# Two MoE layers on one core: the second step's gate and up products moved right behind the first step's, and the expert order found earlier

## The chip, the cores and the metric

One Trainium2 chip, one of its cores. The metric is device microseconds of one execution, as the median over runs; smaller is better.

## What is computed

A trunk of two residual layers over 256 tokens of width 1024, in float32. Layer 0 mixes tokens by a convolution module, layer 1 by differential attention. Each mixer is followed by a mixture of 32 gated-MLP experts (four groups of eight; every token takes the best group and in it two experts), and then by a gated per-layer embedding. The mixture, cut to what matters:

```python
for g in range(N_GROUPS):
    hg = jnp.einsum("bsd,edf->bsef", h, w_gate[g])
    ug = jnp.einsum("bsd,edf->bsef", h, w_up[g])
    act = jax.nn.silu(hg) * ug * combine[:, :, g, :, None]
    out = out + jnp.einsum("bsef,efd->bsd", act, w_down[g])
```

One expert has 3 MB of weights: gate 1024x256, up 1024x256, down 256x1024. All 32 experts of both layers are read, some 200 MB of the 244 MB that the kernel reads.

## The kernel before, in words

**Steps.** The function `moe` (from L1024) works through the experts in steps: in layer 0 eight steps of four experts with 32 token places each; in layer 1 eight steps of two experts with 64 places (one of them shares its step in quarters) and four of four. In layer 1 a place stands not for a fixed expert but for a rank of load: experts are sorted by their counts, so that crowded ones get more places. The first six experts have fixed places (three steps); which expert stands at a later place is found on the chip.

**One step u on TensorE**, in program order: `gate_up(u)` (L1138: the products of its experts with gate and up, in two halves over eight channels), `slots(u)` (L1111, L1115: weights and positions by place), `finish_up(u)` (ACT L1147, DVE L1149: silu times up), half of the `dispatch` of a later step pair (L1076: tokens gathered by a product with the one-hot matrix S, written out by ACT L1081), `combine(u-1)` (L1184), `turn(u)` (L1157, L1159: transposes), `down(u)` (L1170). In the first step of a layer, other work is written between the two halves of `gate_up(0)`: `weights` (L583 to L602), `counts` (L569, L575, and ACT L577, L578), the second half of the first dispatch, and in layer 1 `places_of` (L631 to L643: the sort on DVE). Behind the second half, layer 1 has `by_place` (L649 to L668: ranks, counts and weights are rearranged by place, and the sorted list of experts is written to `row`), then the weight stream is released and `overflow` is prepared.

**The weight stream.** All large weights come through one ring of 16 slots of 1 MB, in one fixed list of tiles, all issued from SP's queue (class `Stream`, L144 to L238). A gate/up tile holds half of the channels of one expert's gate and up (two DMAs of 0.5 MB), a down tile the whole of its down weights. The list is in the order of the steps as they were: a step's gate/up tiles, its down tiles, the next step's gate/up tiles. Slots are handed on strictly in that order:

```python
    while self.used in self.over:
        self.used += 1
    self.fill()
```

so a tile read out of order gives its slot to nobody until all tiles listed ahead of it are read too. Three half tiles of each layer's first step lie in extra buffers (`early`) outside the ring. Counted from a layer's first expert tile, the list is:

- layer 0: tiles 1 to 5 gate/up of step 0, 6 to 9 its down; 10 to 17 gate/up of step 1, 18 to 21 its down; 22 to 29 gate/up of step 2, and so on, twelve a step.
- layer 1: tile 1 gate/up of step 0, 2 and 3 its down; 4 to 7 gate/up of step 1, 8 and 9 its down; 10 to 15 step 2; tiles 16 to 19 gate/up of step 3, 20 and 21 its down; 22 to 25 gate/up of step 4, and so on. From tile 16 on the expert is found by the sort: the list is held there (`W.held`) until `by_place` has written `row`, which SP then reads into a register (L257).

Tile n + 16 can be issued when tiles 1 to n have been read. Other lines used below: L438 `warm` (products for nothing, to keep TensorE going), L552 `low` (DVE: the low parts of the tokens, in halves), L560 `ranks`, L601 and L602 `split_weights`.

Of the kernel before, what the change touches and what calls it, by code (L numbers as in the profile page):

```python
# [10 lines left out]
F32 = mybir.dt.float32  # L11
# [4 lines left out]
AF = mybir.ActivationFunctionType  # L16
# [3 lines left out]
P = 128  # L20
T = 256
D = 1024
NC8 = 8
NE = 32
# [31 lines left out]
RW = ((6, 4), (4, 4))  # L56
# [33 lines left out]
def kernel(  # L90
# [7 lines left out]
    nc = tc.nc  # L98
# [5 lines left out]
    work = ctx.enter_context(tc.tile_pool(name="work", bufs=1))  # L104
# [5 lines left out]
    def ps_b(name="psb"):  # L110
        return psum.tile([P, 512], F32, tag="b", name=name, bufs=2)
# [128 lines left out]
    W = Stream()  # L240
# [107 lines left out]
    ident = const.tile([P, P], F32, name="ident")  # L348
# [85 lines left out]
    def warm(n):  # L434

        ps = ps_b("warm") if n else None
        for _ in range(n):
            nc.tensor.matmul(ps, ones_bf, before[:, None, :].to_broadcast([P, 4, P]), start=True, stop=True)  # L438
# [10 lines left out]
    def routing(i):  # L449


        R = Routing()
# [4 lines left out]
        both = range(2)  # L457
# [9 lines left out]
        cnt = t([P, NE], F32, "cnt")  # L467
# [96 lines left out]
        def counts():  # L564
            pst = ps_b()
            for tt in range(2):
                for t in range(tt + 1):
                    for n in range(2):
                        nc.tensor.matmul(pst[0:NE, tt * P:(tt + 1) * P], oh[:, t, n],  # L569
                                         before_off if t == tt else ones_bf, start=(t == 0 and n == 0),  # L570
                                         stop=(t == tt and n == 1))
            pcn = ps_b()
            for t in range(2):
                for n in range(2):
                    nc.tensor.matmul(pcn[:, 0:NE], ones_bf, oh[:, t, n], start=(t == 0 and n == 0),  # L575
                                     stop=(t == 1 and n == 1))
            nc.scalar.activation(srT, pst[0:NE, 0:T], AF.Copy)  # L577
            nc.scalar.activation(cnt, pcn[:, 0:NE], AF.Copy)  # L578

        def weights():  # L580

# [62 lines left out]

        def by_place():

            pt = ps_b()
            for tt in both:
                nc.tensor.transpose(pt[0:NE, tt * P:(tt + 1) * P], wgt[:, tt], ident)  # L649
            wT = work.tile([NE, T], F32, tag="sq", name="wgtT", bufs=1)  # L650
            nc.scalar.activation(wT, pt[0:NE, 0:T], AF.Copy)
            pm = ps_b()
            for tt in both:
                nc.tensor.matmul(pm[:, tt * NE:(tt + 1) * NE], srT[:, tt * P:(tt + 1) * P], R.permb[:, 0], start=True,
                                 stop=True)
            nc.tensor.matmul(pm[:, 2 * NE:4 * NE], ones_bf[0:NE], R.permb[:, 1:3].rearrange("e a r -> e (a r)"),
                             start=True, stop=True)
            for tt in both:
                nc.tensor.matmul(pm[:, (4 + tt) * NE:(5 + tt) * NE], wT[:, tt * P:(tt + 1) * P], R.perm, start=True,
                                 stop=True)  # L660
            row = t([1, NE], I32, "row")
            nc.vector.tensor_copy(row, pm[0:1, 3 * NE:4 * NE])
            order["row"] = row
            nc.vector.tensor_copy(sr.rearrange("p t e -> p (t e)"), pm[:, 0:2 * NE])
            R.of = late([P, NE], F32, "of")
            nc.scalar.activation(cnt, pm[:, 2 * NE:3 * NE], AF.Copy)
            nc.scalar.activation(R.of, pm[:, 3 * NE:4 * NE], AF.Copy)
            nc.scalar.activation(wgt.rearrange("p t e -> p (t e)"), pm[:, 4 * NE:6 * NE], AF.Copy)  # L668
            split_weights()

        def overflow():
# [15 lines left out]

        R.prepare, R.gather, R.rows, R.logits, R.pick, R.low = prepare, gather, rows, logits, pick, low
        R.ranks, R.counts, R.weights, R.overflow = ranks, counts, weights, overflow
        R.place_constants, R.places_of, R.by_place = place_constants, places_of, by_place  # L690
        return R

    class Pools:
# [22 lines left out]
    pools = [Pools(i) for i in range(2)]  # L716
# [307 lines left out]
    def moe(i, R, between):  # L1024
# [4 lines left out]
        with ExitStack() as ctx:  # L1029
# [54 lines left out]
            def dispatch_first(tt, c0, c1):  # L1084

                if tt == 0 and c0 == 0:
                    hgs[0] = big_t("hg")
                    start.extend(ps_d()[:, 0:256] for _ in range(4))
                for xx in (R.xh, R.xl):
                    for c in range(c0, c1):  # L1090
                        nc.tensor.matmul(start[c], xx[tt][:, c], Ss[0][:, tt],
                                         start=(tt == 0 and xx is R.xh), stop=(tt == 1 and xx is R.xl))
                for c in range(c0, c1):
                    if tt == 1:
                        nc.scalar.activation(hgs[0][:, c], start[c], AF.Copy, scale=g_ffn[:, c:c + 1])
# [111 lines left out]
                dispatch_first(0, 0, 4)  # L1207
            warm(RW[i][0])
            R.ranks(1)
            warm(RW[i][1])  # L1210
            spots(0, (1,))
            R.low(1, 0)
            dispatch_first(1, 0, 4)
            R.low(1, 1)
            for u in range(ns + 1):
                q = u // 2 + 1
                if u == max(OVER_AT[i] - 1, 0):
                    W.ahead = OVER_AHEAD[i]
                if u < ns:
                    gate_up(u, 0, 4)  # L1220
                    if u == 0:
                        R.weights()
                        R.counts()
                        if i == 0:
                            spots(1)
                        dispatch(0, 1)
                        if i:
                            R.places_of()
                        else:
                            R.overflow()  # L1230
                    gate_up(u, 4, 8)
                    if u == 0:
                        pools[i].rest()
                        ep = pools[i].second
                        if i:
                            R.by_place()
                            spots(1)
                            W.held = None
                            W.fill()
                            R.overflow()  # L1240
                    slots(u)
                    finish_up(u)
                    if q < ns // 2:
                        dispatch(q, u % 2)
                        if u % 2 == 1 and q + 1 < ns // 2:
                            spots(q + 1)
                if u:
                    combine(u - 1, 0)
                if u < ns:
                    turn(u)  # L1250
                else:
                    ple_begin(i)
                if u:
                    combine(u - 1, 1)
                if u == OVER_AT[i]:
                    over.loop()
                    W.ahead = RING
                    W.fill()
                between(u, ep)
                if u < ns:  # L1260
                    down(u)
# [696 lines left out]
```

## Time and profile before

| | |
|---|---|
| runs, median (lowest to highest) | 816.93 us (814.59 to 819.43), 3 runs |
| the profiled execution's own time | 815.6 us, of which the span of its instructions is 813.9 us |
| mean granted TensorE clock | 0.944 of 2.4 GHz |
| busy: TensorE matmul / DVE / ACT / POOL | 86% / 48% / 37% / 16% of the span |
| moved by DMA | 246.29 MB, mean 303 GB/s |
| layer 0's experts on TensorE | 155.7 us to about 375 us |
| layer 1's experts on TensorE | 545.3 us to about 782 us |

Times in rows are microseconds from the span's start. In a timeline a row gives start, duration, engine, line, operation, out<-in, count of merged instructions, and in brackets how long the engine stood idle before it and who released it; SPq rows are DMA issues on SP's queue. A row of the windows view gives a stretch, its length, the busy time of each engine (with instructions), then the granted TensorE clock as a share of full speed, the mean busy share of the 16 DMA engines, and GB/s. A row of the waits view gives engine, line, whom it waited for: total us, times, longest.

### The profile page before, as it was taken

The page shows a single profiled execution, that of the slowest core. Times are in us where ns is not written, and L with a number is a line of the kernel's source. Part 1 is how long each engine was busy: PE and PEld are TensorE (multiplying, and loading weights), DVE is VectorE, ACT ScalarE, POOL GpSimd, SP SyncE. Part 2 cuts the span into 40 slices and gives each one's busy share as a digit, 9 for nine tenths or more (in the row PEclk, how much of TensorE's full clock was granted, in tenths as well). Part 3 has the DMA queues.
Part 4 walks back from the last instruction along what each step waited for, and adds up shares of the span by engine and source line. Part 5 has one row for each costly group of instructions (what it writes and reads, how often), then busy time and mean ns, then how long its engine had stood idle before and what let it go on. Part 6 is the DMA issues. An engine that isn't in the chain of part 4 may idle for free.

```text
span 813.9 us, 11540 instructions
## 1 busy us (share of the span) xinstructions
PE 699.6 (86%) x4038; PEld 423.5 (52%) x4038; DVE 389.4 (48%) x1018; ACT 297.8 (37%) x668; POOL 128.6 (16%) x195
## 2 busy tenths in 40 slices
PE   5999968897786778779999898988999999877796
PEld 3788656643331333225898786764445444422255
DVE  3699975622220521217767886572334324202174
ACT  1577723521110212007656666452212212210064
POOL 1487862000000000001013342100000000000011
PEclk9899989999998989879999999997999999999899
DMA  6990365789999999999854128672899999999951
GB/s 186 337 395 9 89 270 166 282 331 405 411 416 413 409 415 410 413 400 376 264 185 155 54 104 307 249 272 104 332 404 397 412 412 411 412 410 413 416 205 52
DMA packets 76112, 246.29 MB, mean 303 GB/s; under 512 B 8626, under 2 KB 29811, under 8 KB 67602
## 3 DMA queue, kind: packets, MB, share of 16 engines
q1 hardware_dynamic: 75906, 245.24, 78.7%
q8 instruction: 34, 0.56, 0.3%
q10 hardware_dynamic: 144, 0.26, 0.1%
q14 instruction: 28, 0.23, 0.1%
HBM read 244.43 MB, written 1.05 MB: 302 GB/s over the span
## 4 chain that ended last, share of the span: by engine, by line
PE 27%; DMA 12%; DVE 7%; ACT 5%; issue 1%; SPq 0%; POOL 0%; POOLq 0%; ACTq 0%; DVEq 0%
PE psa L1138 7%; DMA wslot<-in_moe_w_up_dram 5%; PE psd L1170 4%; DMA wslot<-in_moe_w_down_dram 4%; PE psb L1076 3%; DMA wslot<-in_ple_w_gate_dram 2%; PE psa L430 2%; DVE wslot L189 2%; PE psa L431 2%; PE psa L432 2%; PE psd L1184 2%; DMA wslot<-in_moe_w_gate_dram 1%; ACT e L1649 1%; ACT wslot L173 1%; PE psc L431 1%
## 5 line engine op out<-in xcount | busy, mean ns | idle before, releaser
L1138 PE MATMUL psa<-wslot,hg 128*32 128x512 f32 (+1 forms) x1008 | 191.5, 675 | 50.1 <-DMA wslot<-in_moe_w_up_dram 49.7
L1138 PEld LDWEIGHTS psa<-wslot,hg 128*32 128x32 f32 (+1 forms) x1008 | 52.5, 127 | 180.1 <-issue 164.2
L1120 DVE TENSOR_REDUCE wc<-psb 32x1 f32<-32x2 f32 (+1 forms) x66 | 10.3, 156 | 208.4 <-PE psb L1115 207.7
L1170 PE MATMUL psd<-wslot,aT 128*32 128x512 f32 (+1 forms) x528 | 82.1, 604 | 9.5 <-DVEq L1404 2.8
L1147 ACT ACTIVATE sg<-psa 128x256 f32<-128x256 f32 x20 | 7.7, 385 | 208.7 <-PE psa L1138 208.7
L1174 DVE TENSOR_TENSOR dl<-psd,dh 128x512 fp32r<-128x512 f32 x40 | 27.6, 692 | 88.4 <-ACT dh L1173 88.4
L872 PE MATMUL psa<-hT,wslot 128*128 128x256 f32 x256 | 58.6, 388 | 1.7 <-DVE hT L761 1.7
L1187 DVE TENSOR_TENSOR x<-x,psd 128x512 f32<-128x512 f32 x80 | 50.0, 683 | 16.1 <-PE psd L1184 16.1
L872 PEld LDWEIGHTS psa<-hT,wslot 128*128 128x128 f32 x256 | 49.7, 195 | 9.3 <-DVE hT L761 2.2
L1170 PEld LDWEIGHTS psd<-wslot,aT 128*32 128x32 f32 (+1 forms) x528 | 21.5, 117 | 59.8 <-issue 45.3
L1173 ACT ACTIVATE dh<-psd 128x512 fp32r<-128x512 f32 x40 | 23.8, 597 | 78.4 <-PE psd L1170 78.4
L387 POOL TENSOR_SCALAR rstd<-ss 128x1 f32<-128x1 f32 x7 | 3.0, 424 | 294.8 <-ACT sq L394 293.9
L821 DVE SCALAR_TENSOR_TENSOR chain<-vp,wT,chain 128x256 f32<-128x256 f32 x119 | 48.0, 483 | 0.2
L1076 PE MATMUL psb<-S,xh 128*128 128x256 f32 x144 | 40.0, 310 | 4.5 <-DVE st L1126 2.2
L430 PE MATMUL psa<-wslot,hTa 128*128 128x256 f32 x144 | 43.5, 302 | 0.0
L1081 ACT ACTIVATE hg<-psb,gains 128x256 f32<-128x256 f32 x72 | 30.3, 471 | 33.5 <-PE psb L1076 33.3
L431 PE MATMUL psa<-wslot,hTa 128*128 128x256 f32 x144 | 41.4, 287 | 0.0
L432 PE MATMUL psa<-wslot,hTa 128*128 128x256 f32 x144 | 41.3, 287 | 0.0
L796 ACT ACTIVATE prod<-vp,wT 128x256 f32<-128x256 f32 x83 | 35.9, 498 | 12.6 <-POOL vp L786 6.8
L1076 PE MATMUL psb<-S,xl 128*128 128x256 f32 x144 | 36.7, 287 | 0.0
L801 POOL TENSOR_TENSOR part<-part,prod 128x256 f32<-128x256 f32 x51 | 35.4, 735 | 0.0
L189 DVE TENSOR_TENSOR wslot<-wslot 128x512 fp32r<-128x512 f32 x39 | 33.4, 885 | 2.7 <-ACT wslot L188 2.7
(344 smaller groups left out, 1340.8 us busy)
## 6 DMA issues: line engine op xcount, KB each, us to landing
wslot<-in_moe_w_down_dram SPq DMA_DIRECT2D x64, 1024.0 KB
wslot<-in_moe_w_gate_dram SPq DMA_DIRECT2D x122, 512.0 KB
wslot<-in_moe_w_up_dram SPq DMA_DIRECT2D x122, 512.0 KB
wslot<-in_conv_w_pw_dram SPq DMA_DIRECT2D x12, 1024.0 KB
wslot<-in_da_w_qkv_dram SPq DMA_DIRECT2D x12, 1024.0 KB
wslot<-in_ple_w_gate_dram SPq DMA_DIRECT2D x8, 1024.0 KB
wslot<-in_da_w_o_dram SPq DMA_DIRECT2D x4, 1024.0 KB
early<-in_moe_w_gate_dram SPq DMA_DIRECT2D x6, 512.0 KB
```

Of the source, the lines that this page charges most:

```text
L189: eng.tensor_tensor(lo, w, hi.bitcast(F32), op=ALU.subtract)
L430: nc.tensor.matmul(ps, h[:, 0, c], wh, start=first, stop=False)
L431: nc.tensor.matmul(ps, h[:, 0, c], wl, start=False, stop=False)
L432: nc.tensor.matmul(ps, h[:, 1, c], wh, start=False, stop=last)
L796: nc.scalar.activation(pr, vps[j][:, k:k + T], AF.Copy, scale=wT[:, j, k:k + 1])
L801: nc.gpsimd.tensor_tensor(part[:, n % 2], part[:, n % 2], pr, op=ALU.add)
L821: nc.vector.scalar_tensor_tensor(pc[n], vps[j][:, k:k + T], wT[:, j, k:k + 1], pe if start else pc[n], op0=ALU.mult, op1=ALU.add)
L872: nc.tensor.matmul(pws[j][:, (1 - half) * T:(2 - half) * T], W.get("pw1", j // 2, 1 - half)[:, c, j % 2 * P:(j % 2 + 1) * P], hT[:, c], st ...
L1076: nc.tensor.matmul(ps[:, c * 256:(c + 1) * 256], xx[tt][:, cc], S[:, tt], start=(n == 0), stop=(n == 3))
L1138: nc.tensor.matmul(ps[at:at + width], hg[:, c, s1:s1 + width], w[:, :, c % 4], start=(c == 0), stop=(c == 7))
L1170: nc.tensor.matmul(pd[at:at + w], aT[:, c, at:at + w], W.get("down", i, e)[:, c, k * 512:(k + 1) * 512], start=(c == 0), stop=(c == 1))
L1187: nc.vector.tensor_add(x[:, tt, ks], x[:, tt, ks], ps)
```

## The change

In both layers `gate_up(1)` is written right behind `gate_up(0)`, ahead of `slots(0)`, `finish_up(0)`, `dispatch(1, 0)`, `turn(0)` and `down(0)`. In layer 1, `counts` takes the place of the second `warm`; its copies to SBUF (`keep_counts`, a function of its own now, with `cnt` ahead of `srT`) and the sort `places_of` stand behind the first dispatch, ahead of the second `low`; `by_place` stands behind the first half of `gate_up(0)`, with the release of the weight stream, and `weights` behind that; the weights by place are split off as `turn_weights` (ahead of `gate_up(1)`) and `weights_by_place` (between its halves). The list of tiles is the same. In layer 0 only `gate_up(1)` and the order of the two copies move.

```diff
+            R.counted = pst, pcn
+
+        def keep_counts():
+            pst, pcn = R.counted
+            nc.scalar.activation(cnt, pcn[:, 0:NE], AF.Copy)
             nc.scalar.activation(srT, pst[0:NE, 0:T], AF.Copy)
-            nc.scalar.activation(cnt, pcn[:, 0:NE], AF.Copy)
...
+        def turn_weights():
+            pt = ps_b()
+            for tt in both:
+                nc.tensor.transpose(pt[0:NE, tt * P:(tt + 1) * P], wgt[:, tt], ident)
+            R.wT = work.tile([NE, T], F32, tag="sq", name="wgtT", bufs=1)
+            nc.scalar.activation(R.wT, pt[0:NE, 0:T], AF.Copy)
+
+        def weights_by_place():
+            pm = ps_b()
+            for tt in both:
+                nc.tensor.matmul(pm[:, tt * NE:(tt + 1) * NE], R.wT[:, tt * P:(tt + 1) * P], R.perm, start=True,
+                                 stop=True)
+            nc.scalar.activation(wgt.rearrange("p t e -> p (t e)"), pm[:, 0:2 * NE], AF.Copy)
             split_weights()
...
             R.ranks(1)
-            warm(RW[i][1])
+            if i:
+                R.counts()
+            else:
+                warm(RW[i][1])
             spots(0, (1,))
             R.low(1, 0)
             dispatch_first(1, 0, 4)
+            if i:
+                R.keep_counts()
+                R.places_of()
             R.low(1, 1)
+            gate_up(0, 0, 4)
+            if i:
+                R.by_place()
+                W.held = None
+                W.fill()
+                R.weights()
+            else:
+                R.weights()
+                R.counts()
+                R.keep_counts()
+            spots(1)
+            dispatch(0, 1)
+            if i == 0:
+                R.overflow()
+            gate_up(0, 4, 8)
+            pools[i].rest()
+            ep = pools[i].second
+            if i:
+                R.turn_weights()
+            gate_up(1, 0, 4)
+            if i:
+                R.weights_by_place()
+            gate_up(1, 4, 8)
+            if i:
+                R.overflow()
             for u in range(ns + 1):
...
                 if u < ns:
-                    gate_up(u, 0, 4)
-                    if u == 0:
-                        R.weights()
-                        R.counts()
-                        if i == 0:
-                            spots(1)
-                        dispatch(0, 1)
-                        if i:
-                            R.places_of()
-                        else:
-                            R.overflow()
-                    gate_up(u, 4, 8)
-                    if u == 0:
-                        pools[i].rest()
-                        ep = pools[i].second
-                        if i:
-                            R.by_place()
-                            spots(1)
-                            W.held = None
-                            W.fill()
-                            R.overflow()
+                    if u > 1:
+                        gate_up(u, 0, 8)
                     slots(u)
```

## Rows read from the trace of the kernel before

**Rows 1.** The page's 40 slices of the span: busy tenths of the DMA engines.

```profile
DMA  6990365789999999999854128672899999999951
```

**Rows 2.** The windows view of two long stretches, one in each layer's experts.

```profile
190.00:360.00 170.00, 128.13 (x698) 45.50 (x695) 35.66 (x111) 23.18 (x48) 0.00 (x0) 0.89 1.02 413
578.00:690.00 112.00, 111.51 (x659) 54.24 (x659) 40.48 (x88) 27.46 (x61) 0.00 (x0) 1.00 1.02 408
```

**Rows 3.** The waits of SP's queue from 140 to 400 us.

```profile
SPq L215 <- DMA wslot<-in_moe_w_down_dram: 42.3, 20, 2.2
...
SPq L215 <- PE psd L1170: 8.1, 3, 7.7
```

**Rows 4.** The waits of TensorE from 340 to 376 us, the end of layer 0's experts.

```profile
PE psa L1138 <- DMA wslot<-in_moe_w_up_dram: 6.8, 5, 1.5
```

**Rows 5.** The timeline of SP's queue in layer 0's first step.

```profile
160.24 6.72 SPq L217 DMA_DIRECT2D wslot<-in_moe_w_down_dram  x4
174.58 0.33 SPq L215 DMA_DIRECT2D wslot<-in_moe_w_gate_dram  x1
```

**Rows 6.** The timeline of TensorE in layer 0's first two steps.

```profile
166.56 0.39 PE L1111 MATMUL psb<-wgt_hl,S 128*128 128x8 f32 x2
...
170.93 3.64 PE L1170 MATMUL psd<-wslot,aT 128*32 128x512 f32 x32 [0.96 <-ACT aT L1159]
174.39 7.05 PE L1138 MATMUL psa<-wslot,hg 128*32 128x512 f32 x64
```

**Rows 7.** The windows view of layer 0 around the restart of the stream.

```profile
174.00:176.00 2.00, 2.00 (x24) 0.61 (x20) 0.90 (x2) 0.60 (x1) 0.00 (x0) 1.00 0.41 135
176.00:186.00 10.00, 9.76 (x83) 5.26 (x76) 3.18 (x11) 2.34 (x6) 0.00 (x0) 1.00 0.88 292
```

**Rows 8.** The timeline of SP's queue in layer 1's first two steps.

```profile
558.15 0.36 SPq L267 DMA_DIRECT2D wslot<-in_moe_w_gate_dram  x1
...
570.97 0.33 SPq L267 DMA_DIRECT2D wslot<-in_moe_w_gate_dram  x1
...
574.40 1.23 SPq L263 DMA_DIRECT2D wslot<-in_moe_w_down_dram  x2
```

**Rows 9.** The windows view of layer 1's first two steps.

```profile
558.00:570.00 12.00, 9.72 (x36) 5.76 (x38) 4.12 (x22) 2.76 (x7) 0.00 (x0) 0.57 0.49 175
574.00:576.00 2.00, 2.00 (x12) 0.64 (x10) 0.00 (x0) 0.00 (x0) 0.00 (x0) 1.00 0.59 205
```

**Rows 10.** The timeline of TensorE in layer 1's first step.

```profile
552.01 3.65 PE L1138 MATMUL psa<-early,hg 128*64 128x512 f32 x16
555.59 0.39 PE L649 MATMUL psb<-ident,wgt 128*32 128x128 f32 x2
...
556.45 0.63 PE L659 MATMUL psb<-perm,wgtT 32*128 32x32 f32 x4 [0.28 <-ACT wgtT L651]
558.58 0.35 PE L1111 MATMUL psb<-wgt_hl,S 128*128 128x4 f32 x2 [1.50 <-DVE wgt_hl L602]
...
565.45 5.49 PE L1170 MATMUL psd<-wslot,aT 128*64 128x512 f32 x16 [0.78 <-ACT aT L1159]
```

**Rows 11.** The timeline of ACT there: first and last of `weights`, then the counts.

```profile
546.22 0.31 ACT L585 ACTIVATE gd<-logit,ng 128x4 f32<-128x4 f32 x1
...
548.57 0.20 ACT L587 ACTIVATE ng<-g 128x1 f32<-128x1 f32 x1
...
549.78 0.17 ACT L578 ACTIVATE cnt<-psb 128x32 f32<-128x32 f32 x1
```

**Rows 12.** The timeline of DVE there: both halves of `low`, first and last of `places_of`.

```profile
543.11 2.30 DVE L552 SCALAR_TENSOR_TENSOR xl<-x,sums,xh 128x512 fp32r<-128x512 f32 x2
...
549.98 0.19 DVE L631 SCALAR_TENSOR_TENSOR oh<-cnt,place_key 128x32 f32<-128x32 f32 x1 [1.03 <-ACT cnt L578]
...
551.44 0.22 DVE L643 TENSOR_SCALAR permb<-perm,place_col 32x32 bf16<-32x32 f32 x1
```

**Rows 13.** The chain that ended last: its change from TensorE to DMA in layer 1.

```profile
682.91 0.37 SPq L267
683.55 9.38 DMA wslot<-in_moe_w_gate_dram
```

More of the change, by code (lines that the diff above doesn't have):

```diff
@@ L645, in by_place @@
         def by_place():
[L647 to L651, printed above, removed]
             pm = ps_b()
-            for tt in both:
-                nc.tensor.matmul(pm[:, tt * NE:(tt + 1) * NE], srT[:, tt * P:(tt + 1) * P], R.permb[:, 0], start=True,
-                                 stop=True)
             nc.tensor.matmul(pm[:, 2 * NE:4 * NE], ones_bf[0:NE], R.permb[:, 1:3].rearrange("e a r -> e (a r)"),
@@ L658, in by_place @@
             for tt in both:
-                nc.tensor.matmul(pm[:, (4 + tt) * NE:(5 + tt) * NE], wT[:, tt * P:(tt + 1) * P], R.perm, start=True,
+                nc.tensor.matmul(pm[:, tt * NE:(tt + 1) * NE], srT[:, tt * P:(tt + 1) * P], R.permb[:, 0], start=True,
                                  stop=True)
@@ L667, in by_place @@
             nc.scalar.activation(R.of, pm[:, 3 * NE:4 * NE], AF.Copy)
-            nc.scalar.activation(wgt.rearrange("p t e -> p (t e)"), pm[:, 4 * NE:6 * NE], AF.Copy)
+        def turn_weights():
[10 more added lines that the diff above has]
+            nc.scalar.activation(wgt.rearrange("p t e -> p (t e)"), pm[:, 0:2 * NE], AF.Copy)
             split_weights()
@@ L689, in routing @@
         R.ranks, R.counts, R.weights, R.overflow = ranks, counts, weights, overflow
-        R.place_constants, R.places_of, R.by_place = place_constants, places_of, by_place
+        R.place_constants, R.places_of, R.by_place, R.keep_counts = place_constants, places_of, by_place, keep_counts
+        R.turn_weights, R.weights_by_place = turn_weights, weights_by_place
         return R
```

## The prediction

> **What bounds the kernel now.** I began with the page's 40 slices. The DMA engines are full in two long stretches, one under each layer's experts, and half empty at the head of each [rows 1]. So the question for a change at those heads is whether the weight stream or TensorE sets the pace behind them.
>
> The windows view answers for layer 0: over 170 us the DMA engines are busy all the time at 413 GB/s, while TensorE is idle for 42 us of them [rows 2]. The waits of SP's queue say the same from the other side: the issues for down tiles alone waited 42.3 us in 20 waits behind earlier transfers, against 8.1 us for `down`, of which 7.7 is one wait at the head [rows 3]. To the last step TensorE still waits for up tiles [rows 4]. What the stream loses at the head of layer 0, nothing behind it gives back: the embedding, attention and layer 1 follow in series.
>
> At that head the mechanism is plain. After `gate_up(0)` has freed five slots, SP issues up to tile 21, the last four as one group at 160.24; the next issue stands at 174.58 [rows 5], just when `down(0)` ends (170.93 + 3.64 = 174.57) [rows 6]. The stream is dry at that point: from 174 to 176 the DMA engines are busy for 0.41 of the time [rows 7].
>
> In layer 1 the hold ends at 558.15, but only two tiles can go out; tile 18 follows at 570.97, again at the end of `down(0)` (565.45 + 5.49 = 570.94) [rows 8, 10]. In between the stream stands still for most of 12 us, and TensorE runs at a granted clock of 0.57, mostly the lower of its levels, after standing idle for 1.50 us for the weights by place [rows 9, 10]. From 578 the DMA engines are full again, at 408 GB/s [rows 2].
>
> **The change, part by part.** *The second step's products, layer 0.* The list of tiles is not changed: tiles 6 to 9 (`down(0)`) stand ahead of 10 to 17 (`gate_up(1)`). Reading 10 to 17 early therefore frees nothing. Tile 22 still waits for the end of `down(0)`, and that now has 64 more products ahead of it, 7.05 us [rows 6]. Nothing shortens the way from `slots(0)` to `down(0)`: its waits are for DVE and ACT steps that hang on `slots(0)` itself. `cnt` ahead of `srT` makes the dispatch wait for one more copy, 0.17 us [rows 11]. So SP's next issue moves from 174.58 to 181.8, **+7.2 us**. Behind that one waiting issue on SP's queue stand all further weights, and `gate_up(2)` waits for them. Data for `gate_up(1)` are no problem: its last tile was issued ahead of the four at 160.24.
>
> The bounds: the restart after the gap was slow before, 292 GB/s from 176 to 186 instead of 413, which is 2.9 us lost [rows 7]. If twelve slots freed at once make a better restart, the term falls to 4.3; I take 7.2, since SP's queue was fed in that stretch too and yet slow. It can't be under 4.3 while 413 is the stream's own rate.
>
> *Layer 1, the earlier order.* `counts` replaces four warm products, at no cost while the dispatch behind it waits for S anyway. The sort can start when ACT has written `cnt`; ACT has the four evictions of the first dispatch ahead of it, which ended just before 546.22 [rows 11]. From there: `cnt` 0.17, the sort 551.66 - 549.98 = 1.7, half of `low` 1.15 [rows 12], two short copies some 0.4. So `row` is there at about 549.7 instead of 557.3, and tiles 16 and 17 go out some 7.5 us earlier. That is worth nothing: tile 18 needs the end of `down(0)` in either order, so these two transfers only move within an idle stretch.
>
> *Layer 1, what stands ahead of `down(0)`.* `weights` keeps ACT for 548.77 - 546.22 = 2.55 us [rows 11]. It was hidden under the first half of `gate_up(0)`; now it starts at about 550.2, behind the sort and the two copies, and on ACT the evictions of `dispatch(0, 1)` queue behind it, for which TensorE waits. The second half of `gate_up(0)` then starts at 550.2 + 2.55 + one eviction and the start, 0.65 = 553.4 instead of 552.01 [rows 10]. From there: 3.65 for that half, 0.39 for the transposes, 0.63 for the weights by place [rows 10], 7.05 for `gate_up(1)` as in layer 0, and `slots(0)` to the end of `down(0)` as layer 0 did it at full clock, 174.57 - 166.56 = 8.0 [rows 6]. That gives 573.1, against 570.94: the idle gap and the slow clock are gone (before, the same stretch took 570.94 - 558.58 = 12.4), but the products put in cost more. **+2.2 us** for tile 18.
>
> Against it, six slots come free at once, where before tiles 20 and 21 waited for 574.40 [rows 8] and the stream starved: 205 instead of 413 GB/s from 574 to 576 [rows 9], 1.0 us. Sum for layer 1 **+1.2**, with bounds -1.2 (no delay from ACT, and the 1.0 gained) and +5.6 (the slow clock comes again, 12.4 - 8.0 = 4.4 us more). I take 1.2, the rows at full clock: the slow stretch came behind some 3 us in which TensorE did almost nothing [rows 10], and the new order has no such place, only a gap of about 2 us ahead of the second half.
>
> `overflow` and `spots(1)` run on DVE beside the products in both orders; nothing on POOL is passed, and on SP only the read of `row` moves.
>
> **Sum.** 7.2 + 1.2 = 8.4 us. On the profiled execution 815.6 + 8.4 = 824.0; its own time stands 1.3 below the median of the runs shown, so for the median 816.9 + 8.4 = 825.3, say **825 us**. A measurement of this kernel tells about 0.5% from no change, that is 812.8 to 821.0. The forecast's own bounds: 816.9 + 4.3 - 1.2 = 820.0, and 816.9 + 7.2 + 5.6 = 829.7.
>
> **The rivals.** *TensorE sets layer 1's pace.* The chain that ended last runs on TensorE until 682.91 and only then on DMA [rows 13], and TensorE is busy for 111.5 of 112 us [rows 2]. Once `gate_up(1)` is done, before stood at 570.94 + 7.05 = 578.0 and the new order stands at 573.1 with the same work left: -4.9 us in layer 1 instead of +1.2. Together with layer 0: 816.9 + 7.2 - 4.9 = 819.2. Against it: the DMA engines are busy 1.02 in that very stretch [rows 2], and the transfer at 683.55 takes 9.38 us [rows 13], so it stood behind others: the stream had a queue. Chance 0.15.
>
> *The slow clock comes back in layer 1*, from the new gap behind `weights` on ACT or from the four warm products that are gone: 816.9 + 7.2 + 5.6 = 829.7. For it: a TensorE gap did bring it on there before [rows 9, 10]. Chance 0.12.
>
> *Faster: the stream's rate is paced by free slots and not its own.* Then twelve slots at once let layer 0's stream catch up, TensorE's way decides in both layers, and only layer 1's -4.9 is left: 812.0. It decides from the point where the stream can make up 7.2 us in 170, that is 413 x 170 / 162.8 = 431 GB/s as a mean. Against it speak SP's waits, which are for transfers and not for slots [rows 3]. The Trainium skill ("Perfetto Trace Analysis", Roofline) says that a lone core is held by its 16 DMA engines at about 435 GB/s; by that figure there would be just enough room, and the time would be about 812. The 170 us show 413 throughout. Chance 0.08.
>
> That `gate_up(1)` does not really run early is not to be expected: its tokens are gathered by the first dispatch and its PSUM bank is the free one of two.
>
> **How the numbers follow.** The forecast has the remaining 0.65. Slower by over 0.5% (above 821.0): the forecast but for its lowest end, 0.62, and the slow clock, 0.12: 0.74. Within 0.5%: 0.13 of the first rival and 0.03 of the forecast: 0.16. Faster: 0.10, the last rival and the first one's lower tail. The range 819 to 830 takes in the forecast, the slow clock and most of the first rival, and leaves out the faster case.
>
> **What would show it.** Right: in layer 0 the first issue after tile 21 near 181.8, directly at the end of `down(0)`, an empty stretch of some 7 us in the DMA engines from 174 on, and everything from the embedding on about 7 us later. In layer 1 the hold ends near 557.5 (550.3 + 7.2), two tiles go out, and tile 18 follows about 23 us later at the end of `down(0)`, at full clock. Wrong: DMA busy through 174 to 181; a rate well above 413 GB/s behind the gap; or layer 1's experts shorter by five or so.

## The result, and the profile after

The changed kernel takes **807.85 us** (median of 4 runs, 805.64 to 808.47) against 818.18 us for the kernel before beside it (4 runs): a ratio of 0.9874, 95% interval 0.9833 to 0.9916. It is faster by 1.3%, where slower by 1% was forecast, and it lies outside the range. A later comparison gave 807.96 against 817.76, 0.9893 [0.9867, 0.9920]. The profiled execution took 808.47 us, with a span of 806.8 us against 813.9 before.

The lines of the code shift with the diff: `gate_up` is L1148 now (L1138 before), `down` L1180 (L1170), `slots` L1121, `dispatch` L1086, its eviction L1091.

The prediction named one place at which to look first: SP's issue behind tile 21 in layer 0. The timeline of SP's queue in the changed kernel, layer 0's first step, against [rows 5]:

```profile
170.00 0.33 SPq L215 DMA_DIRECT2D wslot<-in_moe_w_gate_dram  x1
...
174.25 0.33 SPq L215 DMA_DIRECT2D wslot<-in_moe_w_gate_dram  x1
```

And the timeline of its TensorE there, against [rows 6]:

```profile
166.37 7.14 PE L1148 MATMUL psa<-wslot,hg 128*32 128x512 f32 x64
173.44 0.39 PE L1121 MATMUL psb<-wgt_hl,S 128*128 128x8 f32 x2
...
177.80 3.64 PE L1180 MATMUL psd<-wslot,aT 128*32 128x512 f32 x32 [0.96 <-ACT aT L1169]
```

`down(0)` is late by just what was forecast: it ends at 177.80 + 3.64 = 181.44, where 181.8 was said. But the issue does not wait for it. It stands at 170.00, **half way through `gate_up(1)`**: 166.37 + 7.14 / 2 = 169.94, the end of its first half. Three tiles go out by 174, two DMAs each; the issues from 176 on come 1.2 to 1.3 us apart. So tile 22 got a slot from the first half of `gate_up(1)`, 11 us ahead of `down(0)`.

What the stream makes of it, in the windows view of the changed kernel, against [rows 7] and the first of [rows 2] (the last two columns are the DMA engines' busy share and GB/s):

```profile
174.00:176.00 2.00, 1.76 (x17) 1.59 (x14) 1.50 (x6) 0.78 (x2) 0.00 (x0) 1.00 1.00 410
176.00:186.00 10.00, 8.11 (x66) 4.80 (x65) 3.70 (x11) 4.19 (x11) 0.00 (x0) 1.00 1.02 409
...
190.00:354.00 164.00, 121.55 (x698) 43.22 (x691) 36.24 (x112) 23.18 (x48) 0.00 (x0) 0.94 1.02 413
```

The dry stretch is gone: 410 GB/s where there were 135, then 409 where there were 292. Behind it the stream runs at 413 GB/s as before and no faster. The bytes that did not flow before are worth 2 x (410 - 135) / 413 = 1.3 us and 10 x (409 - 292) / 413 = 2.8 us, together 4.1; the stretch from the layer's first product of `gate_up(0)` to its last gate and up products shrank by 4.0 us (202.1 to 198.1). To the end TensorE still waits for transfers, as in [rows 4]; the waits view of TensorE in the changed kernel, 335 to 372 us:

```profile
PE psa L1148 <- DMA wslot<-in_moe_w_up_dram: 9.2, 6, 1.6
```

Layer 1, the timeline of SP's queue in the changed kernel, against [rows 8]:

```profile
547.18 0.35 SPq L267 DMA_DIRECT2D wslot<-in_moe_w_gate_dram  x1
...
557.37 0.33 SPq L267 DMA_DIRECT2D wslot<-in_moe_w_gate_dram  x1
...
561.51 1.24 SPq L263 DMA_DIRECT2D wslot<-in_moe_w_down_dram  x2
569.11 0.33 SPq L267 DMA_DIRECT2D wslot<-in_moe_w_gate_dram  x1
```

And the timeline of its TensorE, against [rows 10]:

```profile
540.83 1.11 PE L1148 MATMUL psa<-wslot,hg 128*64 128x512 f32 x1
...
543.45 0.73 PE L1148 MATMUL psa<-wslot,hg 128*64 128x512 f32 x1
544.01 0.59 PE L1148 MATMUL psa<-wslot,hg 128*64 128x512 f32 x1
...
549.71 3.72 PE L1148 MATMUL psa<-early,hg 128*64 128x512 f32 x16 [1.54 <-ACT hg L1091]
...
553.69 3.65 PE L1148 MATMUL psa<-wslot,hg 128*64 128x512 f32 x16
...
557.83 3.65 PE L1148 MATMUL psa<-wslot,hg 128*64 128x512 f32 x16
...
565.43 3.65 PE L1180 MATMUL psd<-wslot,aT 128*64 128x512 f32 x16 [0.84 <-ACT aT L1169]
```

The hold ends at 547.18 instead of 558.15, and tile 18 follows at 557.37, at the end of the first half of `gate_up(1)` (553.69 + 3.65 = 557.34): the same rule as in layer 0. The two down tiles go at 561.51, when its second half ends. `down(0)` runs at full clock, 3.65 us instead of 5.49, and the gap of 1.5 us ahead of `slots(0)` is gone; a gap of 1.54 us ahead of the second half of `gate_up(0)` came in its place, as forecast.

The windows view of the changed kernel there, against [rows 9] and the second of [rows 2] (the granted clock is the third column from the end):

```profile
540.00:544.00 4.00, 3.94 (x12) 1.76 (x14) 1.83 (x12) 1.88 (x6) 0.00 (x0) 0.57 0.05 23
...
556.00:558.00 2.00, 2.00 (x14) 0.86 (x12) 0.00 (x0) 0.06 (x1) 0.00 (x0) 1.00 0.00 0
558.00:570.00 12.00, 11.16 (x61) 5.52 (x60) 4.00 (x17) 3.86 (x10) 0.00 (x0) 1.00 0.91 345
...
578.00:690.00 112.00, 109.58 (x658) 51.76 (x658) 38.20 (x81) 25.56 (x57) 0.00 (x0) 1.00 1.00 393
```

From 558 to 570 the DMA engines carry 345 GB/s, where they carried 175, and TensorE's granted clock is 1.00 instead of 0.57. From 578 on they carry less than before, 393 instead of 408 GB/s: the stream is ahead, and free slots come at TensorE's pace (from 530 to 780 SP's queue waits 38.6 us for `down` alone, in 7 waits). The slow clock is not gone altogether: it stands at 540 to 544 now, the rows of `gate_up(0)` above show products of 1.1 us until 543.45 and of 0.59 from 544.01.

The chain that ended last, in the changed kernel, around the place of [rows 13]:

```profile
671.11 7.00 PE psa L1148 x64
...
681.70 10.08 DMA wslot<-in_moe_w_gate_dram
```

As before, layer 1 runs on TensorE's pace up to its eighth step and on the stream from there; the last gate and up products come at 757.47 instead of 764.62. Counted from the layer's first product (540.83, and 545.30 before), that is 216.64 us against 219.32: 2.7 us of the gain are layer 1's own in the profile.

### The profile page after: what moved, and what is told of

It reads as the page before. It is cut to its first block, busy times and chain, and to the rows that moved or that the text cites. A ratio compares the mean times of both kernels' runs of the same rounds, so it can differ in the third digit from the quotient of the medians.

```text
span 806.8 us, 11531 instructions
## 1 busy us (share of the span) xinstructions
PE 692.3 (86%) x4034; PEld 424.6 (53%) x4034; DVE 389.8 (48%) x1018; ACT 297.3 (37%) x668; POOL 128.5 (16%) x195
## 4 chain that ended last, share of the span: by engine, by line
DMA 35%; PE 29%; DVE 9%; ACT 8%; issue 2%; POOL 0%; SPq 0%; POOLq 0%; ACTq 0%; DVEq 0%
DMA wslot<-in_moe_w_up_dram 18%; DMA wslot<-in_moe_w_down_dram 12%; PE psa L1148 10%; PE psd L1180 4%; DMA wslot<-in_moe_w_gate_dram 4%; PE psb L1086 3%; DVE wslot L189 2%; PE psd L1194 2%; ACT wslot L173 2%; PE psa L430 1%; PE psa L432 1%; PE psa L431 1%; PE psd L1024 1%; ACT e L1671 1%; ACT wslot L188 1%
## 5 line engine op out<-in xcount | busy, mean ns | idle before, releaser
L1148 PE MATMUL psa<-wslot,hg 128*32 128x512 f32 (+1 forms) x1008 | 186.7, 643 | 48.4 <-DMA wslot<-in_moe_w_up_dram 48.0
L1148 PEld LDWEIGHTS psa<-wslot,hg 128*32 128x32 f32 (+1 forms) x1008 | 52.7, 122 | 172.3 <-issue 158.3
L1180 PE MATMUL psd<-wslot,aT 128*32 128x512 f32 (+1 forms) x528 | 80.9, 597 | 10.9 <-DMA wslot<-in_moe_w_down_dram 4.7
L882 PE MATMUL psa<-hT,wslot 128*128 128x256 f32 x256 | 61.1, 399 | 2.4 <-DMA wslot<-in_conv_w_pw_dram 2.4
L882 PEld LDWEIGHTS psa<-hT,wslot 128*128 128x128 f32 x256 | 51.4, 202 | 10.6 <-DVE hT L771 2.8
L1180 PEld LDWEIGHTS psd<-wslot,aT 128*32 128x32 f32 (+1 forms) x528 | 22.1, 115 | 59.0 <-issue 43.2
L1091 ACT ACTIVATE hg<-psb,gains 128x256 f32<-128x256 f32 x72 | 30.1, 471 | 39.4 <-PE psb L1086 39.3
L430 PE MATMUL psa<-wslot,hTa 128*128 128x256 f32 x144 | 42.8, 297 | 0.0
L1086 PE MATMUL psb<-S,xh 128*128 128x256 f32 x144 | 38.5, 302 | 4.7 <-DVE st L1136 2.0
L432 PE MATMUL psa<-wslot,hTa 128*128 128x256 f32 x144 | 40.6, 282 | 0.0
L431 PE MATMUL psa<-wslot,hTa 128*128 128x256 f32 x144 | 40.6, 282 | 0.0
L1086 PE MATMUL psb<-S,xl 128*128 128x256 f32 x144 | 35.3, 279 | 0.0
```

The costliest lines, as they stand in the source:

```text
L430: nc.tensor.matmul(ps, h[:, 0, c], wh, start=first, stop=False)
L431: nc.tensor.matmul(ps, h[:, 0, c], wl, start=False, stop=False)
L432: nc.tensor.matmul(ps, h[:, 1, c], wh, start=False, stop=last)
L882: nc.tensor.matmul(pws[j][:, (1 - half) * T:(2 - half) * T], W.get("pw1", j // 2, 1 - half)[:, c, j % 2 * P:(j % 2 + 1) * P], hT[:, c], st ...
L1086: nc.tensor.matmul(ps[:, c * 256:(c + 1) * 256], xx[tt][:, cc], S[:, tt], start=(n == 0), stop=(n == 3))
L1148: nc.tensor.matmul(ps[at:at + width], hg[:, c, s1:s1 + width], w[:, :, c % 4], start=(c == 0), stop=(c == 7))
```

## The experiments

The theory after the result, **A**: a new tile takes the slot whose tile was read first, wherever that one stands in the list. `used`, the counter over the list, only says where in the program SP's issue is written; SP runs its queue on its own and waits for the readers of the slot that the issue was given. So as soon as `gate_up(1)` is written ahead of `down(0)`, its slots are also handed out ahead. The rivals: that the slots still go by the list and the gain is TensorE's (layer 1's pace, the clock, the earlier order of experts), or that the stream caught up. Medians are compared with the kernel before on the same chip, in one set for each of the three groups of runs: 817.64 (20 runs), 817.89 (15) and 817.76 us (17).

### Slots bound to the list

The same edit in both kernels. Tile n takes slot n modulo 16, a buffer of its own, so that tile n + 16 waits for the readers of tile n and for no other:

```diff
         def slot(self, a, b, dt=F32):
-            return ring.tile([P, a, b], dt, tag="w", name="wslot", bufs=RING)
+            self.given = getattr(self, "given", -1) + 1
+            return ring.tile([P, a, b], dt, tag=f"w{self.given % RING}", name="wslot", bufs=1)
```

> The changed kernel, with every tile of the weight list bound to slot (its number modulo 16), so that slots are handed on strictly in list order. Theory A (in the changed kernel a tile takes the slot that was read first, in whatever order the list has it, so tiles 22 to 25 take those of gate_up(1)'s first half): this binding brings back the stall that was forecast: in layer 0 the issue behind tile 21 stands at the end of down(0), 181 to 182 us, and the time is some 8 us above the kernel before, 822 to 828 us. Rival B (the slots are handed on in list order in the changed kernel too, and the gain comes from elsewhere): same as the changed kernel, 808 us, issue at 170.

> Control: the kernel before with the same binding. There tiles are read in list order at the heads of both layers, so A and B both expect no change: 818 us within 0.5%, issue behind tile 21 at 174.6, at the end of down(0).

The changed kernel with bound slots took **826.01 us** (825.02 to 830.40; ratio 1.0120 [1.0096, 1.0145]), the kernel before with bound slots 818.55 us (1.0027 [1.0009, 1.0045]). So the binding costs the old order little, and turns the gain of the new one into the loss that was forecast. The timeline of SP's queue in the changed kernel with bound slots, layer 0:

```profile
184.41 0.33 SPq L220 DMA_DIRECT2D wslot<-in_moe_w_gate_dram  x1
```

The timeline of its TensorE:

```profile
176.39 0.39 PE L1126 MATMUL psb<-wgt_hl,S 128*128 128x8 f32 x2
...
180.76 3.64 PE L1185 MATMUL psd<-wslot,aT 128*32 128x512 f32 x32 [0.96 <-ACT aT L1174]
```

And its windows view:

```profile
176.00:184.00 8.00, 6.79 (x58) 3.60 (x56) 2.12 (x7) 2.55 (x6) 0.00 (x0) 1.00 0.65 267
184.00:186.00 2.00, 2.00 (x18) 1.39 (x14) 0.88 (x4) 0.88 (x2) 0.00 (x0) 1.00 0.21 63
186.00:196.00 10.00, 8.15 (x55) 3.90 (x54) 5.82 (x13) 3.26 (x7) 0.00 (x0) 1.00 0.94 318
```

The issue behind tile 21 stands right at the end of `down(0)` again (180.76 + 3.64 = 184.40), with a dry stream and a slow restart behind it, as the prediction drew it, though later than the 181 to 182 that was expected. Layer 0's stretch from its first product to its last gate and up products is 211.3 us against 204.2 in the control: **+7.1**, forecast +7.2. Layer 1's is 221.1 against 220.55: **+0.55**, forecast +1.2. And 826.01 - 818.55 = 7.5 us, forecast 8.4.

That 7.1 lies so near 7.2 is in part luck, for the binding also changes what stands ahead of layer 0's experts. The convolution module keeps weights in the ring as high and low parts, listed in turn, and the program reads all low parts ahead of the last pass over the high parts. The timeline of SP's queue from 131 to 147 us in the kernel before:

```profile
131.14 0.33 SPq L217 DMA_DIRECT2D wslot<-in_moe_w_down_dram  x1
132.66 0.33 SPq L215 DMA_DIRECT2D wslot<-in_moe_w_gate_dram  x1
...
141.39 0.33 SPq L215 DMA_DIRECT2D wslot<-in_moe_w_gate_dram  x1
```

And in the control, its first issue there, with a row of its windows view:

```profile
144.94 0.33 SPq L218 DMA_DIRECT2D wslot<-in_moe_w_down_dram  x1
...
176.00:186.00 10.00, 9.76 (x83) 5.35 (x76) 3.23 (x10) 2.43 (x6) 0.00 (x0) 1.00 1.01 409
```

In the kernel before, tiles 9 to 12 go out from 131.14 to 135.84, as the low parts are let go, and tiles 13 to 16 from 141.39 on, as the last pass over the high parts (from 140.26) goes through. Bound to the list, tile 9 waits for the high part listed first and goes at 144.94, with the others behind it. From 130 to 146 the DMA engines carry 3 GB/s in the control, against 294 in the kernel before; what was held back still flows at 176 to 186, where the kernel before was short of data (409 GB/s against 292). So the two bound kernels differ in SP's issue by 184.41 - 174.49 = 9.9 us, not by 7.2. In the changed one the late tiles also reach `gate_up(1)`, which waits 1.51 us for a transfer. The pair shows that the sign of the change hangs on the rule for the slots; it does not test the terms of the sum one by one.

The other way round, the rule of A written out by hand. Slot numbers go through a queue; a tile that has been read puts its number at the end, a new tile takes the first:

```diff
         def slot(self, a, b, dt=F32):
-            return ring.tile([P, a, b], dt, tag="w", name="wslot", bufs=RING)
+            k = self.free.pop(0)
+            self.held_by.append(k)
+            return ring.tile([P, a, b], dt, tag=f"w{k}", name="wslot", bufs=1)
...
             if key not in self.early:
                 self.over.add(self.pos[key])
+                self.free.append(self.slot_of[self.pos[key]])
```

> The changed kernel with each tile bound explicitly to the slot that was read first (a queue of slots in the order in which the program reads their tiles). Theory A (this is the rule by which the changed kernel gets its slots): the same as the changed kernel, 806 to 810 us, issue behind tile 21 of layer 0 right behind gate_up(1)'s first half, at 170. If some other rule is at work: a different time, or an issue at another point.

809.61 us (0.9902 [0.9876, 0.9928]) against 807.96 (0.9893 [0.9867, 0.9920]) for the changed kernel in the same group: not to be told apart. The timeline of SP's queue in it:

```profile
170.79 0.33 SPq L224 DMA_DIRECT2D wslot<-in_moe_w_gate_dram  x1
```

The issue stands where the changed kernel has it. The trace holds no addresses of slots; A is shown by these two bindings, of which one gives the changed kernel's behaviour and the other brings the forecast's issue and its loss.

### Each layer alone

`gate_up(1)` is put behind `gate_up(0)` in layer 0 alone (everything else as before), or in layer 1 alone, there with the earlier order:

```diff
-            gate_up(1, 0, 4)
...
+            moved = MOVED[i]
+            if moved:
+                gate_up(1, 0, 4)
...
-                    if u > 1:
+                    if u > (1 if MOVED[i] else 0):
                         gate_up(u, 0, 8)
```

> The change in layer 0 alone (layer 1 in the order of before). A: the stream goes on without a gap from 170, which gives 4 us by the last gate and up products of layer 0 (353.85 against 357.76): 814 us. Rival C (all of the gain is in layer 1, from the order found earlier): 818 us.

> The change in layer 1 alone (layer 0 in the order of before). A: the rest of the gain, 3 to 6 us: 812 to 815 us. Rival C: all of it, 808 us.

Layer 0 alone: 812.52 us (0.9941 [0.9919, 0.9962]), -5.1 us. Layer 1 alone: 812.87 us (0.9950 [0.9932, 0.9968]), -4.8 us. Together that is -9.9, and both at once gave 807.96 - 817.76 = -9.8: the two gains are of like size and add up, as they should where the layers follow in series. The timeline of SP's queue with layer 1 alone shows layer 0 as it was:

```profile
175.10 0.33 SPq L219 DMA_DIRECT2D wslot<-in_moe_w_gate_dram  x1
```

### Layer 1: the move or the earlier order

Layer 0 has the change in both kernels here. In the first, layer 1 has the earlier order of experts but keeps `gate_up(1)` at its old place; in the second it has the move but the old order (`counts`, `places_of` and `by_place` where they were):

```diff
+            first = i and ORDER_FIRST
...
-            if i:
+            if first:
                 R.keep_counts()
                 R.places_of()
```

> Layer 0 as changed; in layer 1 only the counts, the sort and the order are early, gate_up(1) stays behind down(0). Compare layer0_alone (812.5). Theory D (the early order helps by taking TensorE's wait and the slow clock behind it out of the way to down(0), not by its two early tiles): end of down(0) 3 us earlier than in layer0_alone (563.8 against 566.8), time 809.5 us. Rival E (the early order is worth nothing by itself): 812.5 us.

> Layer 0 as changed; in layer 1 only gate_up(1) is moved, ahead of slots(0); counts, sort and order stand where they stood, behind gate_up(0). Theory D and A: tiles 18 and 19 take gate_up(1)'s first slots some 7 us before down(0) ends, TensorE does useful work where it waited: 809 us. Rival F (the move pays only with the early order): 812.5 us or more.

Order alone: 814.81 us (0.9954 [0.9934, 0.9975]), no better than layer 0 alone (0.9941 [0.9919, 0.9962]); theory D had expected 809.5. Move alone: **808.14 us** (0.9870 [0.9848, 0.9892]), the changed kernel's time. So layer 1's gain is the move's, and the earlier order is worth nothing that these runs can tell. The timeline of SP's queue in the kernel with the move alone says why:

```profile
557.80 0.35 SPq L271 DMA_DIRECT2D wslot<-in_moe_w_gate_dram  x1
...
560.69 0.47 SPq L271 DMA_DIRECT2D wslot<-in_moe_w_gate_dram  x1
```

Counted from the layer's first product of `gate_up(0)` (545.86 here, 540.83 in the changed kernel), the hold ends 5.6 us later, at 11.9 instead of 6.4, and yet tile 18 goes out no later, at 14.8 instead of 16.5. In the changed kernel it waits for the first half of `gate_up(1)`; here that half ends at 556.65 + 3.65 = 560.3, and by then the hold is over and SP is just done with the two tiles ahead (their last issue stands at 560.08). All that the earlier order does is to send two tiles sooner. In the kernel with the order alone, whose TensorE stands idle for 0.46 us ahead of the weights by place, for 0.90 us behind them and for 0.93 us in the dispatch behind `slots(0)`, the slow clock came back at the old place. The timeline of its TensorE:

```profile
557.68 0.35 PE L1125 MATMUL psb<-wgt_hl,S 128*128 128x4 f32 x2 [0.90 <-DVE off L689]
...
563.60 6.66 PE L1184 MATMUL psd<-wslot,aT 128*64 128x512 f32 x16 [0.78 <-ACT aT L1173]
570.10 7.03 PE L1152 MATMUL psa<-wslot,hg 128*64 128x512 f32 x32
```

`down(0)` takes 6.66 us instead of 3.65, and tile 18 waits for its end: it goes at 570.29, and `down(0)` ends at 570.26, where theory D had 563.8. With the move, products of `gate_up(1)` stand in those gaps.

### The two blemishes that the change left

The warm products that `counts` replaced are put back ahead of it (`warm(RW[i][1])` in both layers); and `weights` goes behind the second dispatch instead of ahead of it (with `spots(1)`), so that the evictions don't queue behind `weights` on ACT:

```diff
-            if i:
+            first = i and ORDER_FIRST
+            if not first or WARM_KEPT:
+                warm(RW[i][1])
+            if first:
                 R.counts()
-            else:
-                warm(RW[i][1])
...
-                R.weights()
+                if not WEIGHTS_BEHIND:
+                    R.weights()
+                    spots(1)
...
             dispatch(0, 1)
+            if first and WEIGHTS_BEHIND:
+                R.weights()
+                spots(1)
```

> The changed kernel with the four warm products kept ahead of counts in layer 1. If the slow clock that the changed kernel shows from 540 to 543.5 comes from the warm products left out, the first half of gate_up(0) takes 3.6 us again instead of 5.0: 807 us, about 1 less. If not: 808 us or 0.5 more, and the slow clock stays.

> The changed kernel with weights written behind dispatch(0, 1) in layer 1, so that ACT does the evictions first. The gap of 1.54 us ahead of gate_up(0)'s second half goes: 806.5 us if TensorE still sets the pace of layer 1's first steps, 808 if the stream does.

> The changed kernel with both: the four warm products ahead of counts, and weights behind dispatch(0, 1), in layer 1. Each took its wait or slow clock away alone, without a measurable gain. If TensorE's pace in layer 1's first steps decides: 806 us, 2 less than the changed kernel. If the stream decides: 808.

> The changed kernel as it is, beside the others of this call: 808 us, 0.985 to 0.99 of the kernel before.

Each edit does what it says to its place. With the warm products `gate_up(0)` starts at full clock: its first product takes 0.64 us in all six profiles of kernels that have them in layer 1, and 1.08 to 1.12 us in all eight of kernels that have not. With `weights` behind the dispatch the second half of `gate_up(0)` starts without the gap. The timeline of TensorE with `weights` behind the dispatch:

```profile
549.80 3.65 PE L1152 MATMUL psa<-early,hg 128*64 128x512 f32 x16
```

The times hardly follow: 808.37 us (0.9877 [0.9854, 0.9899]) and 809.22 us (0.9896 [0.9874, 0.9918]). Both together gave **806.39 us** (0.9857 [0.9833, 0.9881]; 5 runs from 805.21 to 806.60) against 807.96 (0.9893 [0.9867, 0.9920]; 6 runs from 806.69 to 811.87) for the changed kernel in the same group. It is the best median of the study; the intervals overlap, so that it beats the changed kernel is likely and not shown. Nor do these runs show what a microsecond of TensorE's at this place is worth: each repair takes away about 1.5 us, and alone neither shows it in the time. In the profiles layer 1's stretch to its last gate and up products is 217.4 us (warm products), 214.9 (`weights` behind) and 213.7 (both), against 216.6 and 216.1 in two executions of the changed kernel.

### Every step's products one step ahead

If the move is good for the first step, is it for each? In layer 1, `gate_up(u + 1)` for u from 1 to 6 goes right behind `slots(u)` and the dispatch, ahead of `down(u)`:

```diff
-                    if u > 1:
+                    if u > 1 and not (i and 2 <= u <= 7):
                         gate_up(u, 0, 8)
...
                         if u % 2 == 1 and q + 1 < ns // 2:
                             spots(q + 1)
+                    if i and 1 <= u <= 6:
+                        gate_up(u + 1, 0, 8)
```

> The changed kernel, with gate_up(u + 1) written behind the dispatch of step u, ahead of combine, turn and down, for u = 1 to 6 of layer 1. Slots are read some 2 us earlier in each of these steps. If the empty stretch of the stream at 576 to 580 and its slow restart cost time: 806 us, 1 to 2 less than the changed kernel. If not: 808.

817.17 us (0.9985 [0.9967, 1.0002]): a **miss** on both of its expected times, which gives back the whole gain, 9.2 us above the changed kernel. The chain that ended last in it, one step of layer 1:

```profile
571.02 0.31 PE psb L1125 x2
571.56 1.14 PE psb L1090 x8
572.72 0.85 ACT hg L1095 x2
573.61 1.21 PE psb L1090 x8
574.82 7.02 PE psa L1152 x32
...
584.12 3.58 PE psd L1184 x16
587.71 0.31 PE psb L1125 x2
```

And the same step in the changed kernel's chain:

```profile
578.55 6.87 PE psa L1148 x32
...
585.96 2.22 PE psb L1086 x16
...
590.27 3.58 PE psd L1180 x16
593.85 7.00 PE psa L1148 x64
```

From the end of one `down` to the end of the next it is 587.71 - 571.02 = 16.7 us, against 593.85 - 578.55 = 15.3. In the changed kernel the 16 products of a dispatch run in one piece, 2.22 us. With `gate_up` gone from in front of them, `slots` and the dispatch stand right behind `down`, and TensorE waits between the dispatch's halves for ACT's eviction, 0.85 us in the chain; that is the greater part of the 1.4 us. Six such steps are 8.4 of the 9.2 us. The windows views agree: from 578 to 665 the DMA engines carry 360 GB/s here and 388 in the changed kernel. And in that stretch TensorE waits for no transfer, in either kernel; the waits view of TensorE in this one has a single row:

```profile
PE psb L1090 <- ACT hg L1095: 4.6, 5, 0.9
```

**So a loss of TensorE's in these steps reaches the end one for one**; the stream is not what holds layer 1 there.

## Why the prediction was wrong

**What bounds layer 0: right.** The stream set its pace, and the bytes lost at the head were not given back. In the changed kernel the head loses none, and the layer gains 4.0 us in the profile, 5.1 us in the runs of layer 0 alone.

**The step that failed** is the first of the sum: "Reading 10 to 17 early therefore frees nothing. Tile 22 still waits for the end of `down(0)`". It took the counter over the list for the rule of the slots. The counter decides where the issue stands in the program; behind `down(0)`, that is. But the slot that the issue takes is the one read first among those not taken, and after the move those are the slots of `gate_up(1)`. The timeline shows the issue at 170.00, 11.4 us ahead of the end of `down(0)`; bound to the list the same kernel issues at the end of `down(0)`. The description of the weight stream ahead of the prediction has the same error: it is the issues that keep to the list, not the slots. No row that the prediction shows could tell the two rules apart, since in layer 0's first steps the order of reading and the order of the list were the same; but the trace of the kernel before could, some 25 us earlier. Tiles 9 to 12 went out there from 131.14 to 135.84, before the last reading of the high parts that the list has ahead of them; by the list they go at 144.94 and later, as the control shows. The rule was a fact to be read from that trace or from the code of the ring, one tag with 16 buffers, or else an unknown to be bounded from both sides, and the prediction did neither: it stated it. No rival had layer 0 gain either; the lowest, 812.0, left that layer unchanged.

**The size of the terms: near under that rule, in part by luck.** Bound to the list, layer 0 lost 7.1 us (forecast 7.2) and layer 1 0.55 (forecast 1.2), but the issue moved by 9.9 us, from a stream that was not dry in the control. Layer 1's lower bound of -1.2 takes the 1.0 us off twice: without the delay from ACT, 553.4 - 552.01 = 1.4 us, the term is 1.2 - 1.4 = -0.2.

**Layer 1's first rival was the better reading.** That TensorE sets the pace up to its eighth step was given 0.15, for the reason that DMA was busy 1.02 of that stretch and that the transfer at 683.55 took 9.38 us [rows 2, 13]. Both rows are right, and neither speaks of steps 2 to 7: a stream that runs ahead into free slots is busy too. The view that had settled layer 0, the waits of SP's queue [rows 3], speaks for the rival here, already in the kernel before; two of its rows from 576 to 690 us:

```profile
SPq L267 <- PE psd L1170: 33.2, 6, 6.2
...
SPq L267 <- DMA wslot<-in_moe_w_gate_dram: 3.2, 4, 0.8
```

The issues wait for TensorE's reading and hardly for transfers, and TensorE waits for no transfer in that stretch. The run with `gate_up` one step ahead shows it: 1.4 us more of TensorE in a step are 1.4 us more of time. The rival's size was -4.9 us, and layer 1 alone measured -4.8, which is nearer than the profiles bear out. With `gate_up(1)` and `down(0)` both done, the changed kernel is 4.3 us ahead (569.08 - 540.83 = 28.25 us behind the layer's first product, against 577.81 - 545.30 = 32.51); of that 2.7 us are left at the last gate and up products, and 2.2 with layer 1 alone (217.08 us). With bound slots the rival was not borne out (+0.55): there the stream carried nothing from 568 to 582, and the chain that ended last passes to a transfer of 13.65 us at 703.11.

**The earlier order of experts, worth nothing: right,** though for a reason that only half held. Tile 18 is not tied to `down(0)` but, in the changed kernel, to the first half of `gate_up(1)`, and by the end of that half the hold is over in either order.

**The gap behind `weights`: right** (about 2 us forecast, 1.54 measured); on the chain that ended last stands the table load of ACT inside `weights`, 1.28 us at 547.80. **The slow clock, half right.** It left `down(0)`, as taken, but a new one came at the start of `gate_up(0)`, behind the place where the four warm products had gone. A rival had named these, with the price of the slow `down(0)`, 4.4 us; here the half takes 5.1 us instead of 3.65, and taking that away gave nothing that could be measured.

**The faster rival was right by accident.** It said that the stream would catch up at more than 413 GB/s. It did not: 413 it was, before and after. The Trainium skill ("Perfetto Trace Analysis", Roofline) has a lone core at about 435 GB/s from its DMA engines; one window of 2 us shows 438, and no stretch of over 100 us in the rows here shows more than 413.

**What stays open:** why a profiled execution starts layer 1 some 2 us earlier or later than another of a like kernel, whether the kernel with both repairs is really faster than the changed one, and why neither repair shows alone.

## What to carry to other kernels

Where tiles of one tag share a ring of buffers, ask which read frees the buffer that the next transfer takes; here, moving a read forward moved its slot forward too, whatever the list of transfers said. Where a stream runs dry at the head of a stage, put those products first whose tiles can be let go, and then see that the work behind them (here a dispatch with its evictions) still has products to hide under: the same move, done in each step, lost it all again. A busy share of 1.0 on the DMA engines doesn't say who sets the pace while free slots let the stream run ahead; the waits of the issuing queue and of TensorE say more, and slowing the other engine by a known amount tests it.

## What the hardware did that was not expected

A stream that had stood still came back slowly: 292 GB/s over 10 us in [rows 7], and 318 in the changed kernel with bound slots, against 409 where it did not stop, in the changed kernel as in the control. So a stop cost more than its own length here; why, no run shows.

The lower level of TensorE's clock did not go away with one gap: it stood at 558 to 570 before (granted clock 0.57), at 540 to 544 in the changed kernel (0.57), and at both places with the earlier order alone (0.57 and 0.57), each time behind waits that add up to one or two microseconds. Gaps of the same size, such as the 1.54 us ahead of 549.71, passed without it. The kernel before has a slow stretch ahead of `gate_up(0)` too, at 538 to 542 (0.57), but it was over when the products began.
